# State space loads reordered: u first, then E; CA and lags with two buffers each, half a step ahead

## The chip, the cores and the metric

The kernel runs on one core of a Trainium2 chip. The metric is the device time of one execution in microseconds. The core has TensorE (PE in the rows; PEld is its weight load), VectorE (DVE), ScalarE (ACT), GpSimd (POOL) and SyncE (SP), which here only issues transfers between the main memory (HBM) and the on-chip memory (SBUF). Each engine works through its own instructions in the order in which they stand, and waits where an input isn't there or a buffer isn't free.

## The reference, cut to what matters

One layer of a diffusion trunk over 512 latent tokens with a context of 256 tokens. Behind one input projection stand three branches (a short convolution, a state space layer, neighbourhood attention); they are merged by gates, and a squared-ReLU MLP follows. The change touches the state space layer (S5) alone:

```
h_f = diag_scan(lam_bar[0], s5_drive(ux, b_bar[0])) + exp(lam_dt[0] * steps) * h0_f
h_b = diag_scan(lam_bar[1], flip(s5_drive(ux, b_bar[1]))) + exp(lam_dt[1] * steps) * h0_b
y = real(einsum(h_f, c_mat[0]) + einsum(h_b, c_mat[1])) + d_skip * u
```

There are 32 groups of 16 channels, each with 64 complex states for each of the two directions.

## The kernel before, in words

The state space layer is computed by blocks of 8 tokens: matrices made earlier in the kernel carry a block's inputs to the states (E), from the states to the outputs (C, called CA or `ca`) and from the inputs to the outputs within a block (the lags, `ks`); a scan runs over the blocks. These matrices wait in HBM (`E_d`, `C_d`, `KT_d`), and so do the inputs `U_d`. The groups are taken four at a time, in 8 steps q = 0 to 7. For each step:

- `load` brings E (`et`, 512 KB, two buffers) and the inputs (`u`, 256 KB, four buffers); `load2` brings `ca` (512 KB) and `ks` (four transfers of 64 KB), one buffer each. All are issued by SyncE (L629, L631, L635, L639).
- `table` makes the sines and cosines of the step's rotation (GpSimd, VectorE, ScalarE).
- `states` (L660, L661): TensorE multiplies `et` by `u` into PSUM (`stps`, two buffers).
- `rot1`, `rot2`: VectorE and GpSimd rotate the result into `v`; `scan` (L685): eight scans on VectorE; `back1`, `back2`: VectorE and GpSimd rotate back into `h` (L697 to L700, two buffers).
- `outp` (L707, L709): TensorE multiplies `ks` by `u` and `ca` by `h` into PSUM (`yps`, one buffer); ScalarE copies that to `y`, and SyncE writes it to HBM (L712). `u` of a step is last read here, as are `ca` and `ks`.

`gen_s5b` issues these in a pipeline, two pieces for each t: while step t has its states computed, step t-1 is scanned and put out.

Beside the steps run the units of the other branches, which are 24 or 48 matmuls of 512 columns each (L99 to L101: `ga`, `cv`, `gb`). Their weights are streamed in blocks of 1 MB (`raw`, L144, two buffers, also issued by SyncE). Each half block is split into a high part by ScalarE (`wh`, L173) and a low part by VectorE (`wl`, L176); a block's buffer is free, and the next transfer into it can go, when both of its halves are split.

The instructions don't stand on the engines in the order of the source. A planner (`schedule_with_timeline_sim=True`) reckons with costs and durations of its own, and puts on each engine in turn the ready instruction of the highest priority; the steps of the state space layer have a priority 300 instructions ahead of their place in the source. Once it is planned, the order on an engine is fixed: SyncE's queue stands still while the transfer at its head waits.

Of the kernel before, what the change touches and what calls it, by code (L numbers as in the profile page):

```python
# [75 lines left out]
def trunk(tc, xT, ctxT, cond, condT, vecs, wst, s5p, s5bc, dmat, biasA, outT):  # L76
# [27 lines left out]
    with es:  # L104
# [503 lines left out]
        class S5B:  # L608
# [15 lines left out]
                self.t[name, q] = t  # L624
                return t

            def load(self, q):
                et = self.tl("et", q, [128, 8, 128], bufs=2)
                nc.sync.dma_start(et, E_d[q])  # L629
                u = self.tl("u", q, [128, 4, 128], bufs=4)  # L630
                nc.sync.dma_start(u, U_d[q // 2].rearrange("s (n h g) m -> (s n) h g m", n=16, h=2)[:, q % 2])  # L631

            def load2(self, q):
                ca = self.tl("ca", q, [128, 2, 4, 128], bufs=1)
                nc.sync.dma_start(ca.rearrange("p c g m -> p (c g m)"), C_d[q].rearrange("p c m -> p (c m)"))  # L635
                ks = self.tl("ks", q, [128, 4, 128], bufs=1)
                for g in range(4):
                    a = KT_d[4 * q + g, 0:1, 0:16]
                    nc.sync.dma_start(ks[:, g], bass.AP(tensor=a.tensor, offset=a.offset, ap=[[16, 8], [240, 16], [1, 128]]))  # L639
# [74 lines left out]
        def gen_s5b(sb):  # L714

            ok = lambda q: 0 <= q < 8
            for t in range(-2, 11):

                if ok(t + 2):
                    sb.load(t + 2)  # L720
                if ok(t - 1):
                    sb.load2(t - 1)
                if ok(t - 1):
                    sb.scan(t - 1)
                if ok(t):
                    sb.states(t)
                if ok(t - 1):
                    sb.back1(t - 1)
                if ok(t):
                    sb.rot1(t)  # L730
                if ok(t - 1):
                    sb.back2(t - 1)
                yield

                if ok(t):
                    sb.rot2(t)
                if ok(t - 1):
                    sb.outp(t - 1)
                if ok(t + 1):
                    sb.table(t + 1)  # L740
                yield
# [423 lines left out]
        s5f_cm = tc.tile_pool(name="s5f", bufs=1, side="right")  # L1165
        sb = S5B(s5f_cm.__enter__(), s5b_cm.__enter__())
        gs = gen_s5b(sb)
        gens.append(gs)
        ahead[gs] = 300
# [95 lines left out]
        for h, cs in enumerate(HALF):  # L1265
# [3 lines left out]
            for d in range(8):  # L1269
                t = lp.tile([128, 256], F32, tag="o", bufs=4, name=f"hx2t{d}_{h}")  # L1270
# [192 lines left out]
```

## Time and profile before

| | |
|---|---|
| time, median of 3 runs | 1039.29 us (1039.24 to 1041.62) |
| profiled execution | 1037.95 us |
| its span | 1036.2 us, 13604 instructions |
| TensorE busy | 995.4 us (96%) |
| VectorE, ScalarE, GpSimd busy | 571.1, 378.4, 206.5 us |
| mean granted clock of TensorE | 0.981 of 2.4 GHz |

The span reaches from the first to the last instruction of the profiled execution; the execution's own time is 1.75 us longer. Busy time counts the time in which an engine has an instruction running; matmuls overlap, so that a busy TensorE isn't yet TensorE at its peak. A granted clock of 1.00 is 2.4 GHz, 0.50 is 1.2 GHz; a value between them is a mean over a stretch in which both occurred.

### The profile page before, as it was taken

What the parts mean: (1) busy time and instruction counts of PE and PEld (TensorE: products, weight loads), DVE (VectorE), ACT (ScalarE), POOL (GpSimd) and SP (SyncE); (2) the same over time, 40 slices, a digit from 0 to 9 for tenths busy, and PEclk for the clock granted to TensorE, in tenths of its full rate; (3) what the DMA queues carried; (4) which work ended last, traced back from release to release, by engine and by line L of the source; (5) the groups of instructions that cost most, each with busy time, mean ns of one, the idle gap of its engine ahead of it and who ended that gap; (6) DMA issues with size and microseconds to landing.
All of it is one profiled execution on the core that took longest, in us unless ns stands there. A gap on an engine that the chain in (4) does not pass through costs nothing.

```text
span 1036.2 us, 13604 instructions
## 1 busy us (share of the span) xinstructions
PE 995.4 (96%) x5386; PEld 818.4 (79%) x5386; DVE 571.1 (55%) x947; ACT 378.4 (37%) x610; POOL 206.5 (20%) x163
## 2 busy tenths in 40 slices
PE   7799999899799999999999999999999999999997
PEld 4456888788688787878878788998888888888887
DVE  6833599447874144676587885665432324443322
ACT  5223433333222233565465443444421214342311
POOL 0566223475753123210210200000000000000000
PEclk8999999999889999999999999999999999999999
DMA  9425345965455566443354564223232232232202
GB/s 363 163 105 169 131 164 171 227 223 173 164 180 175 163 249 234 135 145 107 114 157 144 199 241 165 82 76 128 82 113 91 82 112 91 82 122 82 82 1 82
DMA packets 64543, 149.38 MB, mean 144 GB/s; under 512 B 28864, under 2 KB 41152, under 8 KB 52064
## 3 DMA queue, kind: packets, MB, share of 16 engines
q1 hardware_dynamic: 47792, 138.99, 38.9%
q10 hardware_dynamic: 16688, 9.53, 3.2%
q8 instruction: 42, 0.69, 0.3%
q14 instruction: 21, 0.17, 0.0%
HBM read 130.16 MB, written 18.32 MB: 143 GB/s over the span
## 4 chain that ended last, share of the span: by engine, by line
PE 76%; DVE 7%; DMA 7%; POOL 4%; ACT 3%; issue 2%; SPq 1%; DVEq 0%; ACTq 0%; POOLq 0%
PE m L99 10%; PE m L100 10%; PE m L101 10%; DMA raw<-in_wst_dram 4%; PE mod L514 2%; DMA C_d<-c 2%; PE ops L836 2%; PE gb L99 1%; PE wo L99 1%; PE wo L100 1%; PE wo L101 1%; DVE wl L176 1%; PE gb L100 1%; PE yps L709 1%; PE gb L101 1%
## 5 line engine op out<-in xcount | busy, mean ns | idle before, releaser
L176 DVE TENSOR_TENSOR wl<-raw,wh 128x1024 fp32r<-128x1024 f32 x144 | 193.7, 1346 | 218.4 <-ACT wh L173 207.5
L173 ACT CAST wh<-raw 128x1024 fp32r<-128x1024 f32 x144 | 151.0, 1050 | 321.0 <-PE m L100 150.9
L99 PE MATMUL m<-rg,wh 128*128 128x512 f32 (+1 forms) x480 | 184.2, 385 | 0.0
L101 PE MATMUL m<-rg,wl 128*128 128x512 f32 (+1 forms) x480 | 183.9, 384 | 0.0
L101 PEld LDWEIGHTS m<-rg,wl 128*128 128x128 f32 x480 | 90.1, 188 | 19.1
L99 PEld LDWEIGHTS m<-rg,wh 128*128 128x128 f32 x480 | 89.9, 188 | 18.6
L100 PE MATMUL m<-rg,wh 128*128 128x512 f32 (+1 forms) x256 | 96.4, 378 | 0.0
L100 PE MATMUL m<-actl,wh 128*128 128x512 f32 x224 | 87.8, 392 | 0.0
L1082 POOL TENSOR_TENSOR junk<-raw,silx 128x1024 f32<-128x1024 f32 x16 | 45.5, 2844 | 196.3 <-DMA raw<-in_wst_dram 188.7
L100 PEld LDWEIGHTS m<-rg,wh 128*128 128x128 f32 x256 | 48.0, 188 | 8.6
L100 PEld LDWEIGHTS m<-actl,wh 128*128 128x128 f32 x224 | 42.0, 187 | 9.8
L514 PE MATMUL mod<-raw,cs 128*2 128x256 f32 x128 | 34.0, 425 | 6.3 <-DVE modc L526 4.3
L1037 DVE SCALAR_TENSOR_TENSOR fg<-m,mod,fg 128x512 f32<-128x512 f32 x14 | 10.5, 751 | 52.8 <-PE m L101 52.8
L685 DVE TENSOR_TENSOR_SCAN v<-r,v 128x96 f32<-128x96 f32 x64 | 28.9, 515 | 11.7 <-POOL v L677 11.7
L92 ACT CAST rg<-relu 128x512 fp32r<-128x512 f32 (+1 forms) x36 | 20.3, 575 | 38.6 <-DVE relu L1030 38.6
L1086 DVE SCALAR_TENSOR_TENSOR jk<-raw,silx 128x1024 bf16<-128x1024 f32 x16 | 21.8, 1360 | 21.1 <-DMA raw<-in_wst_dram 21.1
L93 DVE TENSOR_TENSOR actl<-relu,rg 128x512 fp32r<-128x512 f32 (+1 forms) x36 | 22.3, 632 | 18.5 <-ACT rg L92 18.5
L100 PE MATMUL wo<-rg,wh 128*128 128x256 f32 (+1 forms) x104 | 31.8, 309 | 0.0
L99 PE MATMUL wo<-rg,wh 128*128 128x256 f32 (+1 forms) x104 | 31.8, 307 | 0.0
L101 PE MATMUL wo<-rg,wl 128*128 128x256 f32 (+1 forms) x104 | 31.5, 306 | 0.0
L514 PEld LDWEIGHTS mod<-raw,cs 128*2 128x2 f32 x128 | 11.2, 92 | 25.2 <-issue 11.4
L836 PE MATMUL ops<-pt,v 128*64 128x128 f32 (+1 forms) x256 | 28.3, 294 | 1.2 <-ACT pt L823 1.2
(438 smaller groups left out, 2357.9 us busy)
## 6 DMA issues: line engine op xcount, KB each, us to landing
raw<-in_wst_dram SPq DMA_DIRECT2D x94, 1024.0 KB
E_d<-et ACTq DMA_DIRECT2D x8, 512.0 KB
C_d<-c SPq DMA_DIRECT2D x8, 512.0 KB
et<-E_d SPq DMA_DIRECT2D x8, 512.0 KB
ca<-C_d SPq DMA_DIRECT2D x8, 512.0 KB
fg<-in_xT_dram SPq DMA_DIRECT2D x4, 512.0 KB
raw<-in_wst_dram SPq DMA_DIRECT2D x4, 512.0 KB
u<-U_d SPq DMA_DIRECT2D x8, 256.0 KB
```

The costliest lines, as they stand in the source:

```text
L92: S.copy(hi, src)
L93: (eng or V).tensor_tensor(lo, src, f(hi), op=SUB)
L99: PE.matmul(ps, a[0], b[0], start=start, stop=False)
L100: PE.matmul(ps, a[0], b[1], start=False, stop=False)
L101: PE.matmul(ps, a[1], b[0], start=False, stop=stop)
L173: S.copy(a, src)
L176: V.tensor_tensor(b, src, f(a), op=SUB)
L514: PE.matmul(ps[0:2, 0:256], cs[:, kt], half(h)[:, 256 * (kt % 4):256 * (kt % 4) + 256], start=kt == 0, stop=kt == 7)
L685: V.tensor_tensor_scan(v[:, g, c], r8, v[:, g, c], 0.0, op0=MUL, op1=ADD)
L836: PE.matmul(ops[r], v[:rows, vt, r], pt[:rows, h, t], start=t == 0, stop=t == 3, skip_group_check=True)
L1082: P.tensor_tensor(junk, half(h), silx, op=MUL)
L1086: V.scalar_tensor_tensor(jk, half(h), 1.0, silx, op0=MUL, op1=MUL, accum_out=modx[:, i:i + 1])
```

## The change

The load of E and u is cut in two. In each t, u goes first; E goes later, in the second piece, behind the outputs (in the first two t, which fill the pipeline, it stays with u). `ca` and `ks` get two buffers each, and their load moves from the beginning of a t for step t-1 to the end of a t for step t.

```diff
-            def load(self, q):
+            def loade(self, q):
                 et = self.tl("et", q, [128, 8, 128], bufs=2)
                 nc.sync.dma_start(et, E_d[q])
+
+            def loadu(self, q):
                 u = self.tl("u", q, [128, 4, 128], bufs=4)
...
             def load2(self, q):
-                ca = self.tl("ca", q, [128, 2, 4, 128], bufs=1)
+                ca = self.tl("ca", q, [128, 2, 4, 128], bufs=2)
...
-                ks = self.tl("ks", q, [128, 4, 128], bufs=1)
+                ks = self.tl("ks", q, [128, 4, 128], bufs=2)
...
             for t in range(-2, 11):
 
                 if ok(t + 2):
-                    sb.load(t + 2)
-                if ok(t - 1):
-                    sb.load2(t - 1)
+                    sb.loadu(t + 2)
+                    if t < 0:
+                        sb.loade(t + 2)
                 if ok(t - 1):
                     sb.scan(t - 1)
...
                 if ok(t - 1):
                     sb.outp(t - 1)
+                if t >= 0 and ok(t + 2):
+                    sb.loade(t + 2)
+                if ok(t):
+                    sb.load2(t)
                 if ok(t + 1):
                     sb.table(t + 1)
                 yield
```

## Rows read from the trace of the kernel before

**Rows 1.** The page: span and TensorE's busy time, share, instructions.
```profile
span 1036.2 us, 13604 instructions
...
PE 995.4 (96%) x5386; PEld 818.4 (79%) x5386; DVE 571.1 (55%) x947; ACT 378.4 (37%) x610; POOL 206.5 (20%) x163
```

**Rows 2.** Busy times by stretch: length, five engines, clock, DMA share, GB/s.
```profile
229.00:345.00 116.00, 108.10 (x730) 92.25 (x729) 75.83 (x137) 31.94 (x54) 61.92 (x72) 0.93 0.54 177
...
266.50:273.00 6.50, 6.50 (x34) 5.42 (x35) 5.25 (x8) 0.00 (x0) 6.21 (x8) 0.50 0.01 3
...
283.40:293.20 9.80, 9.75 (x52) 8.97 (x53) 8.72 (x17) 3.15 (x7) 5.13 (x7) 0.50 0.48 146
300.00:341.00 41.00, 41.00 (x271) 35.51 (x270) 18.85 (x36) 9.75 (x16) 14.24 (x18) 1.00 0.58 193
```

**Rows 3.** TensorE's waits, 200 to 360 us: sum, times, longest (us).
```profile
PE stps L660 <- DMA u<-U_d: 4.6, 2, 3.2
PE yps L707 <- DMA ks<-KT_d: 2.3, 2, 1.5
...
PE yps L707 <- ACT tb L650: 0.9, 1, 0.9
```

**Rows 4.** Timeline of TensorE: start, length, instruction, [idle before it and releaser].
```profile
235.87 0.43 PE L707 MATMUL yps<-u,ks 128*128 128x64 f32 x2 [1.50 <-DMA ks<-KT_d]
...
262.45 0.27 PE L660 MATMUL stps<-u,et 128*64 128x96 f32 x1 [1.47 <-DMA u<-U_d]
...
264.08 0.41 PE L707 MATMUL yps<-u,ks 128*128 128x64 f32 x2 [0.92 <-ACT tb L650]
...
281.94 0.27 PE L660 MATMUL stps<-u,et 128*64 128x96 f32 x1 [3.18 <-DMA u<-U_d]
...
283.45 0.66 PE L707 MATMUL yps<-u,ks 128*128 128x64 f32 x2 [0.83 <-DMA ks<-KT_d]
...
297.46 0.43 PE L707 MATMUL yps<-u,ks 128*128 128x64 f32 x2
...
308.33 0.43 PE L707 MATMUL yps<-u,ks 128*128 128x64 f32 x2
```

**Rows 5.** Timeline of SyncE's queue, 234 to 277 us: the issues.
```profile
234.25 11.88 SPq L629 DMA_DIRECT2D et<-E_d  x4
256.10 0.33 SPq L144 DMA_DIRECT2D raw<-in_wst_dram  x1
256.52 0.38 SPq L631 DMA_DIRECT2D u<-U_d  x1
257.00 0.38 SPq L635 DMA_DIRECT2D ca<-C_d  x1
...
258.20 2.48 SPq L639 DMA_DIRECT2D ks<-KT_d  x4
275.72 0.33 SPq L144 DMA_DIRECT2D raw<-in_wst_dram  x1
276.15 0.38 SPq L631 DMA_DIRECT2D u<-U_d  x1
```

**Rows 6.** Waits of SyncE's queue, 255 to 285 us.
```profile
SPq L144 <- DVE wl L176: 24.3, 2, 14.4
```

**Rows 7.** Timeline of VectorE: scans of steps 1 and 6, one low half.
```profile
248.35 4.81 DVE L685 TENSOR_TENSOR_SCAN v<-r,v 128x96 f32<-128x96 f32 x8 [1.72 <-POOL v L677]
...
274.50 1.20 DVE L176 TENSOR_TENSOR wl<-raw,wh 128x1024 fp32r<-128x1024 f32 x1
...
306.41 2.90 DVE L685 TENSOR_TENSOR_SCAN v<-r,v 128x96 f32<-128x96 f32 x8 [2.34 <-POOL v L677]
```

**Rows 8.** Timeline of GpSimd: h of steps 1, 4 (ends) and 6 (beginning).
```profile
258.34 0.74 POOL L700 TENSOR_TENSOR h<-B 64x256 f32<-64x256 f32 x1
...
293.38 0.74 POOL L700 TENSOR_TENSOR h<-B 64x256 f32<-64x256 f32 x1
...
311.31 0.91 POOL L697 TENSOR_TENSOR h<-A 64x256 f32<-64x256 f32 x1 [3.94 <-PE yps L709]
```

## The prediction, on record before the result

> **What bounds the kernel now.** I read the page first: TensorE is busy for 995.4 of 1036.2 us [rows 1], so the kernel is bound by TensorE, and a change elsewhere pays only where it takes away an idle stretch of TensorE or a stretch at the lower clock. Then the busy times by stretch. The state space stage that the diff touches runs from 229 to 345 us: TensorE is busy for 108.10 of its 116 us, and the mean granted clock is 0.93; two stretches inside it stand at 0.50, that is 1.2 GHz, one of 6.5 us and one of 9.8 us. From 300 us on TensorE has no gap and the full 2.4 GHz [rows 2]. So all that can be won lies before 300 us: 7.9 us idle (116 less 108.1), and half of 6.5 and of 9.8 us, 3.25 and 4.90 us, at half clock. Together 16 us, 1.5% of the time, and that is the ceiling. The waits of TensorE name who ended the idle time: loads of u (4.6 us), loads of ks (2.3 us) and one wait put down to a table on ScalarE (0.9 us) [rows 3].
>
> The timeline puts them in order [rows 4]: 1.50 us for ks of step 0 at 235.87; 1.47 us for u of step 4 at 262.45; 0.92 us before the output matmuls of step 1 at 264.08; 3.18 us for u of step 5 at 281.94; 0.83 us for ks of step 2 at 283.45. The 0.92 us I read as ks of step 1 too: the table's result has no part in those matmuls, and the four ks transfers left SyncE between 258.20 and 260.68 [rows 5]. Sum 7.90 us. The two slow stretches each begin right behind such a pair of waits.
>
> Why are u and ks late? SyncE's queue [rows 5]: after the E loads, which run up to step 5 by 246.1, nothing leaves it until a weight block (raw) at 256.10, with u4, ca1 and ks1 behind it; then nothing until the next block at 275.72, again with u5, ca2 and ks2 behind it. The waits of the queue say that both blocks stood at its head until VectorE had made the low halves that free their buffer: 24.3 us in two waits [rows 6]. For the longer one the releaser is the row at 274.50 that ends at 275.70 [rows 7]. u5's own condition, the output matmuls of step 1, is older than that: they began at 264.08 [rows 4], 11.6 us before the block left.
>
> **The change, part by part.** *Two buffers for ca and ks.* ca and ks of step q+1 no longer wait for the output matmuls of step q. The loads stay the same in number, one ca and four ks a step; the four ks cost SyncE 2.48 us of issuing [rows 5], unchanged. Removed: 0.92 us (ks1) and 0.83 us (ks2). The 1.50 us of ks0 stay, since buffer 0 was free before as well. New: ca1 and ks1 may go at the very start, in front of the third E load at 234.25; that puts some 3 us of issuing (2.48 + 0.38 + gaps) in front of it. No wait of TensorE in the stage is put to E [rows 3], so I count nothing, with 3 us as the bound above.
>
> *u first, E behind.* E is loaded far ahead: E of step 5 is issued by 246.1 and first used at 281.94 [rows 4, 5]. Half a step (5.4 us, half of the 10.87 us between the output matmuls of steps 3 and 4, 297.46 and 308.33) is hidden by these 35 us, and so is the write of y that E now queues behind. Without that cover it would cost the 5.4 us in each step. For u the buffers stay at four, so u4 waits for the outputs of step 0 and u5 for those of step 1, as before; the edit alters only what stands in front of u. The planner, not the source, sets the queue's order. In its order the output matmuls of step 1 finish after the low half at 274.50, or u5 would not stand behind that block. The h of step 1 was ready at 259.1 (258.34 + 0.74) [rows 8], so what can have held those matmuls in the plan is ca1 and ks1. With two buffers that reason goes, the plan should set step 1's outputs right behind h1, and u5 in front of the block. So I take the 3.18 us of u5 as removed (bounds: 0 if the order stays, 3.18). The block that then queues behind u5 loses nothing: u5 waits for matmuls that begin by 264.08, the block for a low half that ends at 275.70. For u4, outputs of step 0 are planned as before; I leave its 1.47 us in (bounds 0 and 1.47).
>
> *The clock.* The second slow stretch follows 4.01 us of idle time within 5 us (u5 and ks2). Both go, so I take its 4.90 us as given back (bounds 0 and 4.90). The first follows 1.47 + 0.92 us; one of the two stays, so I take half of its 3.25 us, 1.6 us (bounds 0 and 3.25).
>
> *Sum so far.* 0.92 + 0.83 + 3.18 + 4.90 + 1.6 = 11.4 us of gain.
>
> *What is late next.* The output matmuls need h, which a chain over VectorE and GpSimd makes (rotate, scan, rotate back). In step 4, h was ready at 294.1 and TensorE came at 308.33: 14.2 us of slack [rows 4, 8]. Of these the 11.4 us are used up and 2.8 us are left. Later h wait for TensorE themselves (step 6: 3.94 us for an output matmul [rows 8]), so they come earlier along with it. But the plan will also move outputs forward, as said. If it moves them by x us of other matmuls, TensorE stalls on h for x less 2.8 us, and gets that work back afterwards only as idle time lost. x lies between 0 and one step, 10.9 us; I take the middle, 5.4 us, and so 2.6 us of new stalls. The chain is no faster than before: VectorE's eight scans took 4.81 us at 248.35 beside a busy GpSimd, and 2.90 us at 306.41 [rows 7].
>
> The Trainium skill says in Perfetto Trace Analysis, Optimizing Scalar/DVE Operations, that GpSimd and VectorE share an SBUF read port, so that moving work between them may not help. The two scan rows agree; by that rule a faster TensorE leaves this chain as long as it is; were there no sharing, scans of 2.90 us would end 1.9 us sooner in each step and the 2.6 us would go, a gain of 11.4 us by estimate.
>
> Net: 11.4 - 2.6 = 8.8 us. The memory that the second buffers take and the reordering of the rest of the kernel I cost at nothing: behind 300 us TensorE has no gap to fill and only new gaps could show, which I count in the range at 3 us either way, about the largest single wait of TensorE in the stage [rows 3]. The profiled execution took 1037.95 us (1036.2 us of span and 1.75 us around it), 1.34 us less than the median of 1039.29 us. 1037.95 - 8.8 = 1029.2 for an execution like it; against the median, 1039.29 - 8.8 = 1030.5 us.
>
> **Rivals.** *The loads stay behind the weight block.* If the plan still sets raw before u5, only 0.92 us is sure to go, since the 0.83 us of ks2 would be hidden in a u5 wait of the same length, and the clock falls as before. Gain 0.9 to 2.4 us (with 1.47 us of u4): 1036.9 to 1038.4, no measurable change; up to 3 us worse if the early ca1 and ks1 hold up E2. For it: the diff doesn't touch what frees u, and u4 at least probably stays there. Against it: the queue's order follows the planned end of step 1's outputs, which two buffers move.
> By the Trainium skill (DMA: Bandwidth & Descriptors, Queues, rings and completion order), descriptors of one ring are consumed in ring order. The trace agrees: u4, issued 0.42 us behind a block, was there only 5.9 us later, at 262.45; by this rule it is the place in the queue that counts, and neither the buffers of ca nor those of ks.
>
> *TensorE catches the chain, clock kept.* x = 10.9 us: stalls of 8.1 us, gain 3.3 us: 1036.0, at the edge of what shows.
>
> *Slower: TensorE catches the chain and the clock falls each time.* The same mechanism, with idle stretches of 1 to 2 us in front of each step's outputs, after which the clock stood at 0.50 in the trace of before. Then the 6.5 us that I book for the clock aren't won: 11.4 - 6.5 - (x - 2.8), which turns negative from x = 7.7 us on, and at 10.9 us is a loss of 3.2 us: 1042.5. For it: VectorE and GpSimd are the slowest where they overlap, and a planner that has no such slowing sets the outputs too early. Against it: at steps 0 and 3 to 7 no output matmul waited for h in TensorE's list of waits [rows 3].
>
> **How the numbers follow.** 0.3% of 1039.29 is 3.1 us, which is about what a measurement of this kernel can tell from no change. Chances: my forecast, a gain of 4 to 15 us, 0.52; loads still behind the block 0.20; chain caught with the clock kept 0.13; chain caught with the clock lost 0.15. The forecast is faster by more than 3.1 us throughout. The second rival splits about evenly between faster (0.07) and the same (0.06); the first gives the same 0.17 and slower 0.03; the third the same 0.02, slower 0.13. Faster 0.59, same 0.25, slower 0.16. The forecast's own range: the best case wins 16.0 less the 1.50 us of ks0, 14.5 us: 1024.8; its least, 4 us: 1035.3. Adding 3 us of reordering below and half of the third rival above gives 1022 to 1041, which leaves out the tail of the slower cases.
>
> **What would show it.** Right: in SyncE's timeline ca1 and ks1 leave before 240 us and u5 before the second block; TensorE's waits list ks once (step 0) and u for 1.5 us at most; granted clock 1.00 between 283 and 293; the outputs of step 2 begin near 272 us instead of 283.45. Wrong: u still issued right after a raw block; or new waits of the output matmuls (L709) on GpSimd's h, and again a stretch at 0.50. My prediction fails if the planner's order moves by a whole step, or if weight blocks come late behind a u that waits.

## The result, and the profile after

The changed kernel takes 1045.58 us (median of 5 runs, 1044.29 to 1048.83), the kernel before 1039.29 us beside it: a ratio of 1.0063, with a 95% interval of 1.0034 to 1.0091. It is slower by 6.3 us, where 8.8 us of gain was forecast. One of the five runs of the kernel before took 1637.00 us and is left out of the ratio.

The profiled execution took 1045.52 us. Its page, the same two lines as [rows 1]:

```profile
span 1043.7 us, 13594 instructions
...
PE 999.1 (96%) x5386; PEld 822.3 (79%) x5386; DVE 574.3 (55%) x947; ACT 378.6 (36%) x610; POOL 206.9 (20%) x163
```

TensorE has the same 5386 matmuls. Its waits between 200 and 360 us, beside [rows 3] (outputs are now L709 for ks and L711 for ca, rotating back ends in L701 and L702, state matmuls are L662 and L663):

```profile
PE yps L711 <- POOL h L701: 4.4, 5, 1.9
PE yps L711 <- POOL h L702: 4.3, 4, 1.9
PE ga L99 <- ACT tga L967: 3.0, 1, 3.0
PE gb L99 <- ACT tgb L967: 1.4, 1, 1.4
```

No wait for u or ks is left: all of the 7.9 us of [rows 3] is gone, more than was forecast. (The 1.50 us for ks0 among them are not won: the stage began 2.2 us later, and the first output matmul starts at 236.88 us, where it was 235.87 [rows 4].) In their place stand 8.7 us for h. The busy times by stretch, columns as in [rows 2]:

```profile
205.00:212.00 7.00, 6.14 (x15) 4.84 (x16) 4.24 (x4) 1.74 (x3) 5.57 (x5) 0.52 0.83 300
229.00:345.00 116.00, 107.30 (x718) 91.90 (x717) 78.42 (x136) 31.10 (x53) 63.78 (x72) 0.91 0.54 173
270.00:290.00 20.00, 17.62 (x117) 16.32 (x117) 16.62 (x32) 5.16 (x10) 14.31 (x17) 0.59 0.51 153
300.00:341.00 41.00, 38.25 (x194) 32.04 (x194) 18.74 (x32) 9.35 (x16) 16.59 (x21) 0.96 0.44 137
```

TensorE is busy for 107.30 us of the 116, where it was 108.10, at a clock of 0.91, where it was 0.93. The stretch from 300 to 341 us, which had no gap, now has gaps that sum to 2.75 us. TensorE's timeline says where it waits:

```profile
265.93 0.33 PE L709 MATMUL yps<-u,ks 128*128 128x64 f32 x2
268.21 0.43 PE L711 MATMUL yps<-h,ca 128*128 128x64 f32 x2 [1.95 <-POOL h L701]
269.79 0.69 PE L711 MATMUL yps<-h,ca 128*128 128x64 f32 x2 [1.14 <-POOL h L702]
...
278.15 0.43 PE L711 MATMUL yps<-h,ca 128*128 128x64 f32 x2 [0.43 <-POOL h L701]
280.54 0.69 PE L711 MATMUL yps<-h,ca 128*128 128x64 f32 x2 [1.95 <-POOL h L702]
...
320.36 0.43 PE L711 MATMUL yps<-h,ca 128*128 128x64 f32 x2 [1.26 <-POOL h L701]
321.94 0.43 PE L711 MATMUL yps<-h,ca 128*128 128x64 f32 x2 [0.85 <-POOL h L702]
```

The outputs of step 2 wait 3.09 us, those of step 3 2.38 us, those of step 7 2.11 us. They come early, as was meant: step 2's begin with ks at 265.93 instead of 283.45 [rows 4]. But GpSimd, which makes the last part of h, hasn't got it yet, in steps 2 and 3 here:

```profile
269.01 0.72 POOL L702 TENSOR_TENSOR h<-B 64x256 f32<-64x256 f32 x1
279.75 0.73 POOL L702 TENSOR_TENSOR h<-B 64x256 f32<-64x256 f32 x1
```

10.74 us lie between these two h. From step 1 to step 7 the ends of h stand 9.9 to 11.1 us apart, and in the kernel before 9.6 to 12.5 us; their ends from the first to the last of these span 63.0 us, and 64.9 before. So the chain had about this pace already, and TensorE, coming earlier, runs into it. SyncE's queue, beside [rows 5]:

```profile
232.94 0.45 SPq L637 DMA_DIRECT2D ca<-C_d  x1
233.44 3.67 SPq L641 DMA_DIRECT2D ks<-KT_d  x4
...
249.85 0.33 SPq L144 DMA_DIRECT2D raw<-in_wst_dram  x1
...
263.54 0.32 SPq L633 DMA_DIRECT2D u<-U_d  x1
...
291.44 0.33 SPq L144 DMA_DIRECT2D raw<-in_wst_dram  x1
```

ca1 and ks1 leave at 233 us instead of 257, u5 at 263.54 instead of 276.15, as intended. The weight blocks pay: between 249.85 and 291.44 none leaves, where one left at 256.10 and one at 275.72 [rows 5]. What frees their buffers, the low halves on VectorE, come later:

```profile
247.80 2.02 DVE L176 TENSOR_TENSOR wl<-raw,wh 128x1024 fp32r<-128x1024 f32 x1
...
265.81 1.75 DVE L176 TENSOR_TENSOR wl<-raw,wh 128x1024 fp32r<-128x1024 f32 x1
289.68 1.74 DVE L176 TENSOR_TENSOR wl<-raw,wh 128x1024 fp32r<-128x1024 f32 x1
```

24 us lie between the last two; before, one stood between them, at 274.50 [rows 7]. On VectorE the instructions of the steps, which have priority, now stand in front of them, and the weights of the other branches' units come later.

**What became of the order.** The instructions on TensorE can be counted in their order: how many unit matmuls (L99 to L101) stand between the first state matmuls and the end of each step's outputs.

```
outputs of step             0    1    2    3    4    5    6    7
before                     51   77  110  130  156  182  215  245
after                      51   72   74   76   94  112  136  158
```

The outputs of steps 1 to 3 stand 2 unit matmuls apart from one another. At full clock unit matmuls follow one another every 0.23 us, so that TensorE has about half a microsecond of units between two outputs (and the steps' own matmuls), where the h of the two end 10.74 us apart. At the end of step 7 the outputs are 87 unit matmuls further forward, 20 us. And work that is moved isn't saved: from the last outputs to the last matmul of gb there were 12.9 us before (340.1 to 353.0); now there are 34.2 us (323.8 to 358.0).

Behind the stage a part of the loss is a wait that the profile of before doesn't have, in the list of waits from 345 to 430 us:

```profile
PE v0c L99 <- DVE k L992: 1.7, 1, 1.7
```

### The profile page after: what moved, and what is told of

Read it like the earlier page. It is cut to its first block, busy times and chain, and to the rows that moved or that the text cites. A ratio compares the mean times of both kernels' runs of the same rounds, so it can differ in the third digit from the quotient of the medians.

```text
span 1043.7 us, 13594 instructions
## 1 busy us (share of the span) xinstructions
PE 999.1 (96%) x5386; PEld 822.3 (79%) x5386; DVE 574.3 (55%) x947; ACT 378.6 (36%) x610; POOL 206.9 (20%) x163
## 4 chain that ended last, share of the span: by engine, by line
PE 51%; DVE 3%; DMA 3%; ACT 1%; POOL 1%; issue 1%; DVEq 0%; POOLq 0%; SPq 0%; ACTq 0%
PE m L99 10%; PE m L100 10%; PE m L101 10%; DMA raw<-in_wst_dram 3%; PE wo L99 1%; PE wo L100 1%; PE wo L101 1%; PE ops L842 1%; PE ptps L827 1%; POOL junk L1088 1%; PE m2e L100 1%; PE m2e L99 1%; PE m2e L101 1%; PE na L100 1%; PE na L99 1%
## 5 line engine op out<-in xcount | busy, mean ns | idle before, releaser
L176 DVE TENSOR_TENSOR wl<-raw,wh 128x1024 fp32r<-128x1024 f32 x144 | 190.8, 1326 | 230.6 <-ACT wh L173 225.7
L99 PE MATMUL m<-rg,wh 128*128 128x512 f32 (+1 forms) x480 | 184.2, 385 | 0.0
L101 PE MATMUL m<-rg,wl 128*128 128x512 f32 (+1 forms) x480 | 183.9, 384 | 0.0
L101 PEld LDWEIGHTS m<-rg,wl 128*128 128x128 f32 x480 | 90.1, 188 | 19.1
L99 PEld LDWEIGHTS m<-rg,wh 128*128 128x128 f32 x480 | 90.0, 188 | 18.7
L711 PE MATMUL yps<-h,ca 128*128 128x64 f32 x128 | 24.2, 309 | 8.7 <-POOL h L701 4.4
L99 PE MATMUL wo<-rg,wh 128*128 128x256 f32 (+1 forms) x104 | 31.8, 307 | 0.0
L101 PE MATMUL wo<-rg,wl 128*128 128x256 f32 (+1 forms) x104 | 31.5, 306 | 0.0
L99 PE MATMUL ga<-rg,wh 128*128 128x512 f32 x64 | 26.7, 418 | 3.3 <-ACT tga L967 3.0
```

The source lines that it names most:

```text
L99: PE.matmul(ps, a[0], b[0], start=start, stop=False)
L101: PE.matmul(ps, a[1], b[0], start=False, stop=stop)
L176: V.tensor_tensor(b, src, f(a), op=SUB)
L711: PE.matmul(ps[:, g], ca[:, c, g], h[:, c, g], start=False, stop=c == 1)
```

## The experiments

Theory A: the second buffers let the planner set the outputs of the steps close behind one another; TensorE then waits for the h of each, and the clock falls as it did for u and ks. Rivals: the loss comes from u and E in their new order; a second buffer costs by itself; or VectorE and GpSimd bound the stage in whatever order.

One yardstick serves all of them: the stage from the first state matmul to the last matmul of gb, its length, TensorE's idle time in it, and what the half clock cost (length times one less the mean clock). It stands in a table behind the experiments. Each of its rows is one profiled execution (the mean clock is taken to two digits, so the half clock is good to some 0.6 us), and it can lie some us off the median: *partly_spaced* was profiled at 1038.24 us, its median is 1044.10. The verdicts are the medians and the ratios, each ratio to runs of the kernel before that stood beside it; kernels of different experiments are best compared by their ratios.

**The two halves of the change apart.** *split_only* keeps the split of u and E, and gives ca and ks one buffer each and their old place; *bufs_only* is the kernel before with nothing but

```diff
-                ca = self.tl("ca", q, [128, 2, 4, 128], bufs=1)
+                ca = self.tl("ca", q, [128, 2, 4, 128], bufs=2)
-                ks = self.tl("ks", q, [128, 4, 128], bufs=1)
+                ks = self.tl("ks", q, [128, 4, 128], bufs=2)
```

> Only the split of u and E; ca and ks keep one buffer and their old place. Theory A (the two buffers let the planned order set the output matmuls of the state space steps next to each other, too early for h): the planned order keeps 245 unit matmuls in front of the outputs of step 7, as before, the waits for u and ks stay at 7 to 8 us, the time stays within 3 us of 1039.3. Rival B (u at the head of SyncE's queue, and E later, cost the time): 1044 to 1047 us. Rival C (the loss arises outside the stage, by chance of the plan): anywhere, without waits of the outputs for h.

> Only the two buffers for ca and ks; the load of u and E and the place of the ca and ks load as before. Theory A: 158 unit matmuls in front of the outputs of step 7 instead of 245; no waits for u and ks, 7 to 10 us of waits for h, 1044 to 1048 us like the changed kernel. Rival B: 1036 to 1040, as the order of u and E is that of before.

*split_only*: 1041.54 us, ratio 1.0012 (0.9988 to 1.0036); its outputs stand at 51 to 245 as before. *bufs_only*: 1045.27 us, ratio 1.0063 (1.0034 to 1.0092); its outputs stand at 51, 72, 74, 76 to 158, as in the changed kernel. TensorE's waits from 200 to 360 us, *split_only* first:

```profile
PE stps L662 <- DMA u<-U_d: 6.7, 2, 6.2
PE yps L709 <- DMA ks<-KT_d: 1.5, 2, 1.2
```

```profile
PE yps L709 <- POOL h L700: 4.3, 4, 1.9
PE yps L709 <- POOL h L699: 4.2, 5, 2.0
PE yps L707 <- DMA ks<-KT_d: 2.5, 1, 2.5
```

u first, alone, doesn't take the wait for u away. The buffers, alone, take that wait away, bring the one for h, and give the whole loss. (The 2.5 us for ks are those of step 0.)

**One buffer doubled at a time**: the kernel before with two buffers for ks (*lags_two_buffers_only*) or for ca (*ca_two_buffers_only*), one line of the diff above each.

> The kernel before with a second buffer for the lags (ks) alone. In its planned order 224 unit matmuls stand between the first state matmuls and the last output matmuls of step 7 (245 before, 158 with both second buffers), and 36 between the outputs of steps 1 and 3 (53 before, 4 after). Theory A (the loss comes from outputs planned together ahead of their h): the waits of the outputs for h are between none and the 8.7 us of the changed kernel, 1 to 4 us, and the time stands between the two kernels, 1038 to 1043 us. Rival (a second buffer costs by itself, by the memory that it takes or the transfers that it sets free, whatever the planned order): as slow as with both buffers, 1044 to 1047 us.

> The kernel before with a second buffer for ca alone. In its planned order 210 unit matmuls stand before the end of the outputs of step 7 (245 before, 158 with both), 41 between the outputs of steps 1 and 3. Theory A: waits for h of 1 to 4 us, time between the two kernels, 1038 to 1043 us. Rival (a second buffer costs by itself, and ca is the larger one with 512 KB a step): 1044 to 1047 us.

*lags_two_buffers_only*: 1044.37 us, 1.0039 (1.0005 to 1.0074), above what I expected of theory A and at the lower end of the rival's range. *ca_two_buffers_only*: 1039.04 us, 0.9983 (0.9962 to 1.0005), no change. The waits for h that I expected aren't there (0.3 us, and none). With the lags doubled these are the waits:

```profile
PE yps L707 <- ACT y L711: 5.4, 3, 3.1
PE yps L709 <- DMA ca<-C_d: 3.4, 2, 2.6
```

The outputs, closer together, meet the next single thing: `yps` has one buffer, and ScalarE must have copied the last step's result out of it. In the one for ca a single such wait of 4.2 us stands. There the outputs of the step before were done by 274.7 us, but on ScalarE their copy stands behind the next step's table, which waits for GpSimd:

```profile
285.86 0.52 ACT L649 ACTIVATE tb<-rr 128x384 f32<-128x384 f32 x1 [9.39 <-POOL rr L648]
286.29 0.51 ACT L650 ACTIVATE tb<-rr 128x384 f32<-128x384 f32 x1
286.71 0.35 ACT L711 COPY y<-yps 128x256 f32<-128x256 f32 x1
```

So the theory of h is too narrow. What these traces have in common is that outputs planned closer together than their inputs and their buffer follow make TensorE wait for one or the other; which, depends on the order. That a second buffer costs by itself, whatever the order, is refuted for ca, the larger, and by *two_buffers_spaced* below for both together.

**Spacing the outputs, with VectorE's order.** *spaced_by_low_halves* is the changed kernel with two edits. The scan is kept on VectorE behind the last low half that precedes it in the source (`after` is the kernel's own helper that keeps an instruction behind a named one), and each t from 1 on has one further `yield`, which lets the other branches go on by a piece:

```diff
-                V.tensor_tensor(b, src, f(a), op=SUB)
+                order["wl"] = V.tensor_tensor(b, src, f(a), op=SUB)
...
-                    sb.scan(t - 1)
+                    with after("wl"):
+                        sb.scan(t - 1)
...
                 yield
+                if t >= 1:
+                    yield
```

> The changed kernel with its state space steps spread out: each step's scans stand behind the low half split last in the source, and a step takes three pieces instead of two from t = 1 on, so that 276 unit matmuls come in front of the outputs of step 7 instead of 158. Theory A: waits for h below 3 us, no waits for u or ks in the steps 1 to 7, one slow stretch at most, and a time of 1029 to 1036 us, faster than both kernels. Rival (VectorE and GpSimd bound the stage whatever the order): waits for h as in the changed kernel or longer, 1043 us or more. Rival B: no better than 1044, as u and E stay as changed.

1032.94 us, ratio 0.9945 (0.9921 to 0.9970): faster than both kernels. Its outputs stand at 51, 72, 84, 105, 184, 205, 255 and 276. The time is as expected; the waits for h are 6.2 us in three instead of the less than 3 expected.

*partly_spaced* has the first edit without the `yield`:

> The changed kernel with the scan kept on VectorE behind the last low half that its source precedes, without the further piece of other work in each t. Outputs end at 51, 72, 74, 76, 125, 146, 167 and 188 unit matmuls: steps 1 to 3 stand as close as in the changed kernel (2 apart), steps 4 to 7 are 21 to 49 apart (18 to 24 there). Theory A: the h waits of steps 2 and 3 stay and those of steps 4 to 7 go; time between the changed kernel and the spaced one, 1035 to 1042 us. Rival (only the whole of the spacing, with the further piece, does anything): 1043 to 1047 us.

1044.10 us, ratio 1.0046 (1.0018 to 1.0075), outside what I expected of theory A. Spacing steps 4 to 7 alone wins nothing back that shows. *spaced_outputs_pinned* has both edits and the pin of the next paragraph:

> The spaced version of the changed kernel with the outputs of each step also kept behind the last unit matmul that its source precedes. Outputs end at 51, 72, 84, 105, 179, 200, 246 and 267 unit matmuls (51, 72, 84, 105, 184, 205, 255, 276 without the pin), so little differs. Theory A: h waits of 5 to 8 us, nearly all in steps 1 to 3 (12 and 21 unit matmuls apart, 2.7 and 4.8 us, beside a chain of 10 to 11 us a step), time as the spaced one, 1029 to 1036 us. Rival (the gain of the spaced one was a chance of its order): 1038 to 1046 us.

1035.32 us, ratio 0.9930 (0.9903 to 0.9958), as expected; its h waits are 6.1 us.

**Spacing on TensorE alone.** Is it the place of the outputs, or VectorE's order? *outputs_pinned_only* leaves the scan to the planner and pins the outputs:

```diff
-        PE.matmul(ps, a[1], b[0], start=False, stop=stop)
+        order["mm"] = PE.matmul(ps, a[1], b[0], start=False, stop=stop)
...
-                    sb.outp(t - 1)
+                    with after("mm"):
+                        sb.outp(t - 1)
...
                 yield
+                if t >= 1:
+                    yield
```

> The changed kernel with the outputs of each step kept on TensorE behind the last unit matmul that its source precedes, and the further piece of other work in each t; the scans are not pinned. Outputs end at 51, 72, 74, 101, 137, 173, 209 and 245 unit matmuls: steps 1 and 2 stand 2 apart as in the changed kernel, steps 3 to 7 are 27 to 36 apart. If the place of the outputs decides: one or two h waits of about 2 us at step 2, none later, 1036 to 1041 us. If VectorE's order decides (its scans still go ahead of the low halves): 1043 to 1048 us.

1032.93 us, ratio 0.9943 (0.9921 to 0.9964): the place of the outputs decides; it wins more than expected. The chain is the same up to there: the h of steps 2, 3 and 4 end at 269.47, 280.25 and 290.93 us, in the changed kernel at 269.73, 280.48 and 290.33. Against *partly_spaced* the two waits of step 3 are gone. Waits from 200 to 360 us and the stretch from 270 to 290 us (columns as in [rows 2]), *partly_spaced* first:

```profile
PE yps L711 <- POOL h L702: 4.0, 3, 1.9
PE yps L711 <- POOL h L701: 2.7, 2, 2.1
```

```profile
270.00:290.00 20.00, 15.68 (x117) 14.38 (x117) 11.56 (x21) 5.16 (x10) 11.85 (x14) 0.66 0.53 171
```

The same two views of *outputs_pinned_only*:

```profile
PE yps L711 <- POOL h L701: 2.3, 2, 1.9
PE yps L711 <- POOL h L702: 1.0, 1, 1.0
```

```profile
270.00:290.00 20.00, 20.00 (x143) 17.68 (x144) 17.37 (x32) 5.73 (x10) 13.76 (x16) 0.79 0.40 125
```

Steps 1 and 2 stand 2 unit matmuls apart in both, and both wait for h of step 2. Step 3 stands at 76 in the one, with 4.0 us of waits and a clock of 0.66; at 101 in the other, with no idle time and 0.79. The further `yield` stands in every kernel that gained, beside one pin or the other; no run has it alone with the priority kept, nor the pin of the outputs without it, so which of the two spaces them is not shown.

**Spacing without the change.** *before_spaced* is the kernel before with the scan's edit and the `yield`, *u_first_spaced* the same with u first and E behind, *two_buffers_spaced* the same with the two buffers.

> The kernel before, one buffer each and its loads untouched, with the same two edits that spaced the changed kernel: the scan may stand on VectorE only behind the last low half that its source precedes, and one further piece of other work in each t. Its outputs end at 51, 77, 110, 131, 156, 195, 255 and 285 unit matmuls. If the spacing alone makes the gain of the spaced kernel (1032.9 us): 1030 to 1036 us. If the early loads are needed with it: u and ks still stand behind the weight blocks, 5 to 8 us of TensorE's waits are theirs, and the time is 1037 to 1042 us.

> u first and E behind, one buffer each for ca and ks at their old place, with both spacing edits. Outputs end at 51, 77, 110, 131, 156, 195, 255 and 285 unit matmuls, as in the spaced kernel before. If u's place in the queue costs nothing once the outputs are spaced: 1031 to 1036 us, as the spaced kernel before (1033.7 us), with ks waits of 3 to 5 us. If u first gives back the u waits that it promises: up to 2 us less, 1029 to 1033 us. If it is worth a loss: above 1037 us.

> The kernel before with two buffers each for ca and ks, its loads at their old places, and both spacing edits. Outputs end at 51, 72, 84, 105, 184, 205, 255 and 276 unit matmuls, as in the spaced changed kernel. If the second buffers cost nothing once the outputs are spaced: 1031 to 1036 us. If they cost a part of their 5 us in any order: 1037 to 1042 us.

*before_spaced*: 1033.66 us, 0.9908 (0.9874 to 0.9941). *u_first_spaced*: 1032.15 us, 0.9933 (0.9909 to 0.9958). *two_buffers_spaced*: 1031.94 us, 0.9929 (0.9899 to 0.9960). With *spaced_by_low_halves* (0.9945) all four corners are there, and their intervals overlap: once the outputs are spaced, neither the second buffers nor u's place is worth anything that these runs can tell. In *before_spaced*, with one buffer each, the waits for ks are the only ones over 2 us:

```profile
PE yps L707 <- DMA ks<-KT_d: 4.9, 3, 3.1
```

**No priority for the steps.** *no_priority* is the changed kernel with the further `yield` and `ahead[gs] = 0` instead of 300, so that the planner has no reason to favour the steps.

> The changed kernel with three pieces a step from t = 1 on and without the 300 instructions of priority for the steps: 268 unit matmuls in front of the outputs of step 7, but only 77 and 113 in front of those of steps 2 and 3. Theory A: better than the changed kernel, 1032 to 1041 us, with 2 to 6 us of waits for h, those at steps 1 to 3. Rival (VectorE and GpSimd bound the stage whatever the order): 1043 us or more.

1060.87 us, ratio 1.0210 (1.0177 to 1.0242): the waits for h are gone as expected, the time went the other way. The reason is another one, below (what was not expected).

**Both kernels once more**, to see what of the profiles is the change's:

> The changed kernel once more, to see what of its profile comes back. If the stretch at half clock from 205 to 212 us, ahead of the stage, belongs to the change: again about 0.5 there, and the stage begins 2 us later than before. If it is a chance of the execution: 1.00 there in this one, and the first state matmuls at 232 to 233 us. Theory A: waits for h of 8 to 9 us in any case, and the stage (first state matmuls to last matmul of gb) 122 to 127 us long, beside 120.3 us before.

> The kernel before once more, for the same reason: the waits for u and ks come back, 6 to 8 us, and the stage is 117 to 121 us long. The stretch from 205 to 212 us may stand at 1.00 or at 0.50; either way it is no work of the change. If it is the change's: 1.00.

*after_again* waits 9.1 us for h, and the 1.7 us wait behind the stage comes back (0.4 us in *before_again*). In *before_again* a wait of 6.4 us at step 5's first state matmul is put down to VectorE. u5 left SyncE only at 273.52 us there, behind a weight block, and the matmul began at 279.15, so I read it as the wait for u5; with it the waits for u and ks are 9.0 us, more than the 6 to 8 expected. The stretch from 205 to 212 us stood at a clock of 0.76 there, 0.52 in the first execution and 1.00 in both executions of before; but *bufs_only* and *partly_spaced* have 1.00, *before_spaced* has 0.76. What brings it is not settled; it follows neither the buffers nor the loads.

The stage in all of them, in us:

| kernel | ratio | step 7 ends at | stage | idle | half clock | rest |
|---|---|---|---|---|---|---|
| before; again | 1 | 245 | 120.3; 118.6 | 9.3; 10.4 | 8.4; 7.1 | 102.6; 101.1 |
| after; again | 1.0063 | 158 | 123.1; 124.6 | 10.1; 12.0 | 9.8; 10.0 | 103.2; 102.6 |
| split_only | 1.0012 | 245 | 118.0 | 10.6 | 4.7 | 102.7 |
| bufs_only | 1.0063 | 158 | 126.7 | 12.5 | 11.4 | 102.8 |
| lags_two_buffers_only | 1.0039 | 224 | 123.3 | 11.0 | 8.6 | 103.7 |
| ca_two_buffers_only | 0.9983 | 210 | 117.0 | 8.5 | 4.7 | 103.8 |
| partly_spaced | 1.0046 | 188 | 121.6 | 10.3 | 9.7 | 101.6 |
| outputs_pinned_only | 0.9943 | 245 | 111.9 | 5.8 | 5.6 | 100.5 |
| spaced_outputs_pinned | 0.9930 | 267 | 112.5 | 6.6 | 3.4 | 102.5 |
| spaced_by_low_halves | 0.9945 | 276 | 110.5 | 7.7 | 0.0 | 102.8 |
| two_buffers_spaced | 0.9929 | 276 | 110.2 | 5.9 | 2.2 | 102.1 |
| before_spaced | 0.9908 | 285 | 115.8 | 5.1 | 8.1 | 102.6 |
| u_first_spaced | 0.9933 | 285 | 114.7 | 7.0 | 4.6 | 103.1 |
| no_priority | 1.0210 | 268 | 141.8 | 2.1 | 5.7 | 134.0 |

Apart from *no_priority*, the rest is the same 100 to 104 us of TensorE's work in every one: a stage is that work, its idle time and its half clock. Each of these that is faster than before has 5 to 8 us of idle time, the others 8.5 to 12.5. Step 7's place alone doesn't sort them (245 is before's and *outputs_pinned_only*'s): what else is late, and how closely the outputs stand, counts too.

## Why the prediction was wrong

**The step that failed is the size of x**, by how much the plan moves the outputs forward: "x lies between 0 and one step, 10.9 us; I take the middle, 5.4 us, and so 2.6 us of new stalls". Counted in the order, it is 36 and 54 unit matmuls at steps 2 and 3, where TensorE waits first, 8 and 12 us, and 20 us at step 7, twice the bound; the new stalls are 8.7 and 9.1 us. The bound took the edit for a shift by at most one step. But nothing held the plan there: with ca and ks no longer in the way, each step's outputs move up behind the last, and the error grows from step to step. What the planner reckons for h is in no trace. That the steps stand ahead of the low halves on VectorE, so that fewer units are ready in between, fits steps 4 to 7, which *partly_spaced* moves apart; steps 1 to 3 stand 2 apart there too, so for them the reason stays open. A step's distance in the plan, 2 unit matmuls between the outputs of steps 1, 2 and 3, was the number to bound, beside the 10 to 11 us that the chain takes.

With x fell the term of the clock: the new stalls were charged with their own length alone, and the 6.5 us of clock were booked as won. By the table (two executions of each kernel, which differ between themselves by 1 to 2 us) the idle time, forecast to fall by 2.3 us (4.93 less 2.6), rose by 1.2, and the half clock, forecast to give back 6.5 us, cost 2.2 us more. In the stage the clock is the larger part of the miss.

Point by point:

- *The ceiling and where it lies*: right. The yardstick bears it out: idle time and half clock are nearly all that moves, 17.7 and 17.5 us in the two executions of before.
- *ks1, ks2, u5 go* (0.92, 0.83, 3.18 us): right; *bufs_only* shows that the second buffers alone bring u5 in front of the block (265.81 us, the block 291.98), *split_only* that u's place alone doesn't. One second buffer is enough for that, for ca (265.82) or for ks (266.35), so ca1 and ks1 needn't both be freed, as I had it. u4's 1.47 us went too, which I had left in; ks0's 1.50 us passed into the later start of the stage (0.6 us are back in *after_again*, 2.5 us in *bufs_only*). The first rival, loads that stay behind the block, is refuted with that.
- *The clock, 4.90 and 1.6 us*: wrong. The stretch from 270 to 290 us stands at 0.59. New waits of 1.95 and 1.14 us, and of 0.43 and 1.95 us, took the place of the old ones in front of it. Over the stage the half clock costs 9.8 and 10.0 us, where it was 8.4 and 7.1.
- *E behind costs nothing*: nearly right; *after_again* has one wait of 0.8 us for E.
- *14.2 us of slack of h, and "Later h wait for TensorE themselves ... so they come earlier along with it"*: wrong where the outputs stand close. The h of steps 2 and 3 end at 269.73 and 280.48 us, before at 269.90 and 281.65; they didn't come earlier by more than 1.2 us, while the outputs of step 2 came 17.5 us earlier (265.93 for 283.45).
- *Behind 300 us only new gaps could show, 3 us either way*: there are some in the stage (2.75 us together) and one behind it (1.7 us).
- *The third rival* named the mechanism, its place and its sign, at 0.15; with x bounded at 10.9 us it ended at a loss of 3.2 us. By its own formula the 20 us of step 7 would give 12 us of loss; 6.3 us were measured, since TensorE waits mostly at steps 2, 3 and 7, and not for the whole shift.

Where the time lies: the two profiled executions of each differ by 9.5 us, more than the 6.3 us of the medians. The stage is 4.4 us longer (123.9 less 119.5), the time behind it 2.1 us (685.5 less 683.4, of which the wait for k is 1.3 to 1.7), and the stage began 3 us later (235.0 less 232.0). The last of these isn't settled; the six kernels that are faster than before began theirs at 234.3 to 236.8 us, so it doesn't decide.

The Trainium skill says in Perfetto Trace Analysis, Optimization Strategy, that the same gap coming back on the engine that should be saturated can mean too few buffers. The gaps for ks of steps 1 and 2 before [rows 3] agree: two buffers took them away. That this makes the kernel faster doesn't follow: the gaps came back for h at 8.7 us. The Trainium skill also advises, in Trainium Kernel Development and Optimization, Best Practices, double buffers for performance, to overlap transfers with work; here the second buffers by themselves cost 0.63% (0.34 to 0.92, *bufs_only*) in the plan as it fell out, and made no difference that shows in the spaced one.

## What to carry to other kernels

Where a planner orders in-order engines, a buffer more is a change of the order, not only of a wait: before reckoning what the removed wait is worth, ask what else held the planned instruction back, and count in the new order how much other work is left between two uses of a chain, against the time that the chain takes. If that is less, place the consumers by hand, behind work that is surely ready; here a pin and one more `yield` gave a ratio of 0.9943 where the second buffers without them gave 1.0063. And test the cure on the kernel without the change, too: it was the spacing that gained, not the loads.

## What the runs showed of the hardware that was not expected

**Alternating kinds of matmul is dear.** In *no_priority* TensorE is never idle between 260 and 300 us, at a clock of 1.00, and yet 31 us slower in the stage. Its timeline:

```profile
265.71 0.39 PE L99 MATMUL ga<-rg,wh 128*128 128x512 f32 x1
265.94 0.39 PE L100 MATMUL ga<-rg,wh 128*128 128x512 f32 x1
266.26 0.38 PE L662 MATMUL stps<-u,et 128*64 128x96 f32 x2
266.56 0.49 PE L101 MATMUL ga<-rg,wl 128*128 128x512 f32 x1
266.99 0.38 PE L663 MATMUL stps<-u,et 128*64 128x96 f32 x2
267.30 0.49 PE L99 MATMUL ga<-rg,wh 128*128 128x512 f32 x1
```

Two unit matmuls in a row start 0.23 us apart; two state matmuls and a unit matmul, in turn, take 0.73 to 0.74 us (266.26 to 266.99). In batches two state matmuls, one of each line side by side, take 0.08 us (in *outputs_pinned_only* L662 starts 14 times from 263.80 to 264.87, with L663 right behind each). So each alternation costs about 0.42 us (0.73 less 0.23 and 0.08), or 0.34 us if two of one line, as they stand here, take 0.08 us each. 75 to 90 at this price make the 31 us; counted in the order, 84 pairs of state matmuls stand alone between other matmuls in *no_priority*, and none before or in the changed kernel, where they come in runs of 6 or more. The priority of the steps, which packs the outputs, also keeps these kinds in batches. Which property of the two kinds it is (their data type, or their size) wasn't tried.

**Idle time before the clock falls.** In the changed kernel 0.50 follows two waits of 1.95 and 1.14 us, 1.58 us apart; in *two_buffers_spaced* it falls (0.87, then 0.78 in the next five microseconds) behind a single one of 3.55 us; in *spaced_by_low_halves* waits of 2.87 and 1.42 us, 4.4 us apart, left it at 1.00 throughout. So the idle time booked against an order doesn't tell alone what the clock costs.
